# A two-layer S5 and sparse-attention trunk on one core: transposed activations, gate products and split weights placed lowest in SBUF, one 8 KB room used in turn by three stages

## The chip, the core and the metric

The program runs on one core of one Trainium2 chip. The metric is the device time of one execution in microseconds, the median of several runs. TensorE multiplies matrices, VectorE and ScalarE do elementwise work and move results out of PSUM, GpSimd (POOL) does a few small operations and issues a few DMAs, and SyncE's queue issues nearly all DMAs. SBUF, the on-chip memory, is addressed by partition (128 of them) and by a byte offset in the partition; every tile of this kernel has a range of bytes that is the same in all partitions.

## The reference

The input is 256 tokens of 1,024 float32 values. Two layers each do: half a SwiGLU block, a mixer, half a SwiGLU block. The mixer of layer 0 is an S5 state-space layer, that of layer 1 is a sparse attention with three branches, whose keys and values come from the state after layer 0. Cut to what matters here:

```
def _swiglu(x, w_in, w_out):
    a, b = jnp.split(x @ w_in, 2, axis=-1)
    return (jax.nn.silu(a) * b) @ w_out

for layer in range(2):
    h = h + 0.5 * _swiglu(_rmsnorm(h, ffn1_norm[layer]), ffn1_w_in[layer], ffn1_w_out[layer])
    u = _rmsnorm(h, mix_norm[layer])
    h = h + (_s5_mixer(u, ...) if layer == 0 else _nsa_mixer(u, kv, ...))
    h = h + 0.5 * _swiglu(_rmsnorm(h, ffn2_norm[layer]), ffn2_w_in[layer], ffn2_w_out[layer])
    if layer == 0:
        kv = _shared_kv(h, ...)
```

w_in is 1024 x 5632 and w_out 2816 x 1024. `silu(a) * b` is called the gate product below. In the attention, each branch is a softmax of logits times values; in the S5 mixer, u is multiplied into a small state per group of channels, which is scanned along the sequence.

## The kernel before

All weights stream through the core once. A load brings a *granule* of 1 MB (128 partitions x 2,048 floats) into one of two `raw` buffers. ScalarE rounds it to the 32-bit reduced float type (`whi`), VectorE takes the difference (`wlo`); each has five buffers of 4 KB per partition (lines 86 to 102). Activations are split in the same way, so that one product of float32 accuracy is three matmuls of the reduced type: high activation times high weight, high times low, low times high (`mm3`, lines 118 to 120). In these matmuls the weights are the moving operand, up to 512 columns, and the activations the stationary one, 128 x 128, loaded before each matmul.

A feed-forward block (`ffn`) runs over 11 chunks of 256 hidden columns. For a chunk, 48 matmuls multiply the transposed activations `xT` (16 KB per partition: high and low, 8 slices, 256 tokens) with w_in into the accumulators `mm`. ScalarE and VectorE form the gate product `g` from them (lines 249 and 250). In the next chunk, after its fifth slice, TensorE turns `g` (line 204), and ScalarE and VectorE write the turned product, split into high and low, to `gT` (lines 143 and 144). Then, after that chunk's own 48 matmuls, 24 matmuls multiply `gT` with w_out into the accumulators `o`, which stay for all chunks. So TensorE's order is: 48 on `xT` with four transposes after the 30th, 24 on `gT`, and so on. The four blocks are called block 1 (layer 0, first half) to block 4 (layer 1, second half). Other work is woven in where there is room: S5 preparation in block 1, attention bias tables in block 2, keys and values in block 3. `issue_after` keeps the order on each engine as written.

The S5 stage turns its normalized input into `uT` (8 KB per partition, lines 508 to 516), multiplies it with input matrices (line 527), scans (line 542), and forms the output (lines 557 to 566). Its output, split, goes into the tile `xT` again, for a product with w_glu. In the attention stage, `mix` normalizes the probabilities `Pt`, turns them 128 keys at a time (line 911), copies the turned blocks to `pt0` (ScalarE) and `pt1` (VectorE), two buffers of 2 KB each, and multiplies the values with them (line 920).

Tiles come from pools. A pool takes its bytes above the pools that are open at that time, in the order in which they were opened, and gives them back when it closes. A tile that is allocated again waits for the last user of the bytes that it gets. Open for the whole kernel are, from the bottom up: `pers` (h 8 KB, small constants, `xT` 16 KB), `rawp` (16 KB), `hip` and `lop` (20 KB each: `whi`, `wlo`), and `small`. Above them come the stage's pools: the S5 tables (104 KB) and their scratch in block 1, attention tables and scratch later, and in each block the pool `ffn`, which holds two `g` (2 KB each) and two `gT` (4 KB each). So `xT` starts 9 KB above the first pool's start, `raw` 25, `whi` 41, `wlo` 61; `gT` starts 199 KB above it in block 1, 169 KB in blocks 2 and 3, and 127 KB in block 4.

Of the kernel before, what the change touches and what calls it, by code (L numbers as in the profile page):

```python
# [9 lines left out]
F32 = mybir.dt.float32  # L10
F32R = mybir.dt.float32r
# [5 lines left out]
P = 128  # L17
D = 1024
KT = D // P
FF = 2816  # L20
CHUNKS = ((0, 4, 304), (4, 4, 256), (8, 4, 256), (12, 4, 256))
NCH = FF // 256
# [10 lines left out]
def kernel(ctx: ExitStack, tc: tile.TileContext, A, out):  # L33
    nc = tc.nc
    V, S, G, T = nc.vector, nc.scalar, nc.gpsimd, nc.tensor

    pers = ctx.enter_context(tc.tile_pool(name="pers", bufs=1))
    rawp = ctx.enter_context(tc.tile_pool(name="rawp", bufs=2))
    hip = ctx.enter_context(tc.tile_pool(name="hip", bufs=5))
    lop = ctx.enter_context(tc.tile_pool(name="lop", bufs=5))  # L40
    small = ctx.enter_context(tc.tile_pool(name="small", bufs=2))
    dscr = ctx.enter_context(tc.tile_pool(name="dscr", bufs=1, space=bass.MemoryType.DRAM))

# [5 lines left out]

    def tr_bank():  # L50
        return Banks.tr.tile([P, 512], F32, name=Banks.tag)


    h = pers.tile([P, 2, D], F32, name="h")
# [93 lines left out]
    class Acts:  # L148
        def __init__(self, hc, gain=None):
            self.h, self.gain = hc, gain  # L150
            self.xT = pers.tile([P, 2, KT, 256], F32R, name="xT")
            self.rs = small.tile([P, 2], F32, name="rs", bufs=4)
            self.ss = small.tile([P, 4], F32, name="ss")

# [36 lines left out]
    def ffn(x, gi, w_in, w_out, res, perm=False, bg=None, steps=1, done=None, first=()):  # L191
        with tc.tile_pool(name="ffn", bufs=2) as fp, tc.tile_pool(name="ps_a", bufs=1, space=PSUM) as pa:
            xT, rs = x.xT, x.rs
            acc2 = [[pa.tile([P, 512], F32, name=f"o{t}{hf}") for hf in range(2)] for t in range(2)]
            g_in = granules([w_in[c, kh] for c in range(NCH) for kh in range(2)], gain=gi, first=first)
            g_out = granules([w_out[j] for j in range(NCH)])

            def transposed(g):

                gT = fp.tile([P, 2, 2, 256], F32R, name="gT")  # L200
                ps = tr_bank()
                for f in range(2):
                    for t in range(2):
                        T.transpose(ps[:, (f * 2 + t) * P:(f * 2 + t + 1) * P], g[:, t, f * P:(f + 1) * P], ident)  # L204
                if perm:
                    src = ps.rearrange("p (f t e c) -> p f t e c", f=2, t=2, e=2)
                    hi, lo = (gT[:, i].rearrange("p f (c t e) -> p f t e c", t=2, e=2) for i in range(2))
                    for f in range(2):
                        split(hi[:, f], lo[:, f], src[:, f])
                else:  # L210
                    split(gT[:, 0], gT[:, 1], ps.rearrange("p (f c) -> p f c", f=2))
                return gT

            def second(c, gT):
                if c < NCH - 1:
                    for f in range(2):
                        for hf in range(2):
                            w = next(g_out)
                            for t in range(2):
                                mm3(acc2[t][hf], gT, f, t, w, c + f == 0, False)  # L220
                    return
                ws = [[next(g_out) for _ in range(2)] for _ in range(2)]
                for t in range(2):
                    for hf in range(2):
                        for f in range(2):
                            mm3(acc2[t][hf], gT, f, t, ws[f][hf], False, f == 1)
                        cs = slice(hf * 512, (hf + 1) * 512)
                        V.scalar_tensor_tensor(out=res[:, t, cs], in0=acc2[t][hf], scalar=0.5, in1=res[:, t, cs], op0=ALU.mult, op1=ALU.add)
                        done(t, hf)

            prev = None
            for c in range(NCH):
                acc = [mm_bank() for _ in range(2)]
                gT = None
                if c == 0:
                    gemm(acc, xT, g_in, lead=True)
                else:
                    for k in range(KT):
                        w = next(g_in)
                        for t in range(2):  # L240
                            mm3(acc[t], xT, k, t, w, k == 0, k == KT - 1)
                        if k == 4:
                            gT = transposed(prev)
                        if k % 2:
                            background(bg, steps)
                g = fp.tile([P, 2, 256], F32, name="g")
                for t in range(2):
                    sl = g[:, t, :]
                    Last.act = S.activation(sl, acc[t][:, 0:256], AF.Silu, scale=rs[:, t:t + 1])  # L249
                    Last.dve = V.scalar_tensor_tensor(out=g[:, t, :], in0=acc[t][:, 256:512], scalar=rs[:, t:t + 1], in1=sl,  # L250
                                                      op0=ALU.mult, op1=ALU.mult)
                if c:
                    second(c - 1, gT)
                prev = g
                background(bg, steps)
            second(NCH - 1, transposed(prev))

    BG1 = 1.65  # L260
    NG = 32
    NC = 64
# [221 lines left out]

    def s5(hc, x, W, kp, done):
        cosT, sinT, Cw, Wi, WBT, r4 = W.cosT, W.sinT, W.Cw, W.Wi, W.WBT, W.r4
        with tc.tile_pool(name="s5r", bufs=1) as rp, tc.tile_pool(name="s5w", bufs=2) as wp, \
                tc.tile_pool(name="ps_dr", bufs=2, space=PSUM) as pd, tc.tile_pool(name="ps_y", bufs=2, space=PSUM) as py, \
                tc.tile_pool(name="ps_g", bufs=1, space=PSUM) as pg:
            Banks.tr, Banks.tag = py, "yb"  # L490
            uT = rp.tile([P, NG, NC], F32, name="uT")
            uv = uT.rearrange("p (r a) c -> p r a c", a=2)
            yh = pers.tile([P, 2, KT, 256], F32R, name="xT")
            gacc = [[pg.tile([P, 512], F32, name=f"ga{t}{n}") for n in range(2)] for t in range(2)]
            glu_w = [load_granule(A["w_glu"][j], 512) for j in range(2)]
            gen = granules([A["w_glu"][j] for j in range(KT // 2)], first=glu_w)
# [299 lines left out]
    def attention(x, hc, done):  # L796
        with tc.tile_pool(name="at", bufs=1) as ap, tc.tile_pool(name="at2", bufs=2) as tp, \
# [8 lines left out]
            vcol = ap.tile([P, 1], F32, name="vcol")  # L806
            nc.sync.dma_start(out=vcol, in_=A["valid"])
            xT, rs = x.xT, x.rs
            rsh = ap.tile([P, 2], F32, name="rsh")
            V.tensor_scalar(out=rsh, in0=rs, scalar1=0.5, scalar2=None, op0=ALU.mult)  # L810
            qT = ap.tile([P, 16, 256], F32R, name="qT")
# [84 lines left out]
            def mix(g, t, Pt, sm):  # L896
# [9 lines left out]
                for kb in range(t + 1):  # L906
                    pts = []
                    for br in range(2):
                        ps = tr_bank()
                        for r in range(4):  # L910
                            T.transpose(ps[:, r * P:(r + 1) * P], Pt[:, r, br, kb * P:(kb + 1) * P], ident)  # L911
                        pts.append(tp.tile([P, 512], F32, name=f"pt{br}"))
                        if br:
                            V.tensor_copy(pts[br], ps)
                        else:
                            S.activation(pts[br], ps, AF.Copy)
# [198 lines left out]
```

## Time and profile before

| | before |
|---|---|
| median of three runs | 1060.9 us (1058.21 to 1061.9) |
| profiled execution | 1057.09 us |
| its span (first to last instruction) | 1055.3 us |
| TensorE (PE) busy | 996.1 us, 94% |
| VectorE, ScalarE, GpSimd busy | 669.9, 583.2, 135.8 us |
| mean granted TensorE clock | 0.982 |
| DMA | 171.73 MB, mean 163 GB/s |

A row of the page or of a group gives the line of the code, the engine, the operation, the tiles (written <- read), the number of instructions and the mean time of one. PEld is the load of a stationary operand. A row of the timeline begins with the start in microseconds from the start of the span and the duration; matmuls overlap in it, so the distance from one start to the next (the *step* below), not the duration, is what a matmul costs in a dense stretch. A row of the chain has start, duration, and what ran. A row of a stretch gives from:to, its length, then for PE, PEld, VectorE, ScalarE and GpSimd the busy time and the number of instructions, then the granted clock, the DMA engines' share and GB/s.

### The profile page before, as it was taken

Reading aid. Unit: us, or ns where it says so; the run is one execution under the profiler, and the core shown is the slowest. Engines: PE = TensorE matmul, PEld = TensorE weight load, DVE = VectorE, ACT = ScalarE, POOL = GpSimd, SP = SyncE. Lnnn points to the kernel's source line nnn. Section 1 sums busy time; section 2 is a strip of 40 time slices with the busy share of each in tenths; the row PEclk is TensorE's granted clock in tenths of the full one; section 3 lists DMA queues with packets and bytes.
Section 4 is the critical chain, followed back from the end, with each engine's and each line's share of the span. In section 5 each row is a group of like instructions: output and inputs, shape, how many; then the busy total and the mean of one; then the engine's idle time right before and its main releaser. Section 6 shows DMA issues by size and latency. Waiting matters only on the chain.

```text
span 1055.3 us, 14565 instructions
## 1 busy us (share of the span) xinstructions
PE 996.1 (94%) x5553; PEld 806.6 (76%) x5553; DVE 669.9 (63%) x1258; ACT 583.2 (55%) x1039; POOL 135.8 (13%) x142
## 2 busy tenths in 40 slices
PE   6999999988799799999999999999887999999998
PEld 5888888776577588887887888887865678888886
DVE  4999854367864556566666455555788866556553
ACT  5677675352264555554755555454876755545552
POOL 3001110327611000000013000000205210000000
PEclk9999999989899899999999999999988999999999
DMA  7556554303258755554554455553312145545551
GB/s 256 200 189 211 194 179 147 120 2 112 90 182 240 269 197 179 184 196 160 197 206 156 160 196 170 193 193 115 100 34 91 42 155 199 198 173 188 198 171 70
DMA packets 27910, 171.73 MB, mean 163 GB/s; under 512 B 4544, under 2 KB 4992, under 8 KB 9024
## 3 DMA queue, kind: packets, MB, share of 16 engines
q1 hardware_dynamic: 26192, 164.77, 45.2%
q0 software_dynamic: 1648, 6.03, 2.2%
q8 instruction: 43, 0.70, 0.3%
q14 instruction: 27, 0.22, 0.1%
HBM read 165.54 MB, written 5.24 MB: 162 GB/s over the span
## 4 chain that ended last, share of the span: by engine, by line
PE 80%; DVE 9%; ACT 4%; DMA 3%; POOL 3%; issue 1%; SPq 0%; ACTq 0%; POOLq 0%; DVEq 0%
PE mm L118 15%; PE mm L119 15%; PE mm L120 15%; PE o L118 8%; PE o L119 8%; PE o L120 8%; DMA raw<-in_w_in_dram 3%; PE tr L204 2%; DVE wlo L102 1%; DVE w L542 1%; DVE Pt L904 1%; DVE wlo L90 1%; ACT Pt L893 1%; POOL z L502 1%; PE tr L911 1%
## 5 line engine op out<-in xcount | busy, mean ns | idle before, releaser
L118 PE MATMUL mm<-whi,xT 128*128 128x512 f32 (+2 forms) x800 | 313.3, 392 | 4.0 <-ACT whi L86 2.5
L119 PE MATMUL mm<-wlo,xT 128*128 128x512 f32 (+2 forms) x800 | 306.1, 383 | 0.7 <-DVE wlo L90 0.5
L120 PE MATMUL mm<-whi,xT 128*128 128x512 f32 (+2 forms) x800 | 306.2, 383 | 0.0
L102 DVE SCALAR_TENSOR_TENSOR wlo<-raw,gains,whi 128x512 fp32r<-128x512 f32 (+2 forms) x320 | 221.4, 730 | 111.7 <-ACT whi L99 108.0
L99 ACT ACTIVATE whi<-raw,gains 128x512 fp32r<-128x512 f32 (+2 forms) x320 | 207.4, 694 | 136.1 <-PE mm L120 58.6
L90 DVE TENSOR_TENSOR wlo<-raw,whi 128x1024 fp32r<-128x1024 f32 x140 | 171.0, 1226 | 122.7 <-ACT whi L86 122.6
L86 ACT ACTIVATE whi<-raw 128x1024 fp32r<-128x1024 f32 x148 | 154.5, 1057 | 153.5 <-PE mm L120 58.2
L118 PEld LDWEIGHTS mm<-whi,xT 128*128 128x128 f32 x800 | 150.8, 189 | 35.1 <-ACT whi L86 2.9
L120 PEld LDWEIGHTS mm<-whi,xT 128*128 128x128 f32 x800 | 150.6, 188 | 29.7
L119 PEld LDWEIGHTS mm<-wlo,xT 128*128 128x128 f32 x800 | 150.9, 189 | 28.7 <-DVE wlo L90 1.5
L118 PE MATMUL o<-whi,gT 128*128 128x512 f32 x352 | 140.5, 399 | 10.9 <-ACT gT L143 10.9
L119 PE MATMUL o<-wlo,gT 128*128 128x512 f32 x352 | 139.5, 396 | 0.0
L120 PE MATMUL o<-whi,gT 128*128 128x512 f32 x352 | 138.9, 396 | 0.0
L118 PEld LDWEIGHTS o<-whi,gT 128*128 128x128 f32 x352 | 66.6, 189 | 27.6 <-ACT gT L143 12.6
L120 PEld LDWEIGHTS o<-whi,gT 128*128 128x128 f32 x352 | 66.5, 189 | 16.0 <-DVE gT L144 0.4
L119 PEld LDWEIGHTS o<-wlo,gT 128*128 128x128 f32 x352 | 66.6, 189 | 14.9
L249 ACT ACTIVATE g<-mm,rs 128x256 f32<-128x256 f32 x88 | 41.0, 471 | 28.2 <-PE mm L120 27.9
L250 DVE SCALAR_TENSOR_TENSOR g<-mm,rs,g 128x256 f32<-128x256 f32 x88 | 41.8, 481 | 22.5 <-ACT g L249 22.4
L144 DVE TENSOR_TENSOR gT<-tr,gT 128x512 fp32r<-128x512 f32 (+1 forms) x55 | 36.4, 663 | 27.4 <-ACT gT L143 27.0
L143 ACT ACTIVATE gT<-tr 128x512 fp32r<-128x512 f32 (+1 forms) x55 | 33.3, 606 | 36.1 <-PE tr L204 29.3
L140 POOL TENSOR_TENSOR rs<-ms,nhalf 128x1 f32<-128x1 f32 x12 | 7.2, 600 | 219.9 <-DVE ms L139 219.9
L893 ACT ACTIVATE Pt<-Pt,mx 128x128 f32<-128x128 f32 (+1 forms) x64 | 28.4, 445 | 6.4 <-DVE mx L888 6.4
(300 smaller groups left out, 985.2 us busy)
## 6 DMA issues: line engine op xcount, KB each, us to landing
raw<-in_w_in_dram SPq DMA_DIRECT2D x87, 1024.0 KB, 4.9
raw<-in_w_out_dram SPq DMA_DIRECT2D x44, 1024.0 KB, 4.9
raw<-in_w_kv_dram SPq DMA_DIRECT2D x6, 1024.0 KB, 4.8
raw<-in_w_glu_dram SPq DMA_DIRECT2D x4, 1024.0 KB, 4.8
raw<-in_w_o_dram SPq DMA_DIRECT2D x4, 1024.0 KB, 4.8
revd<-rev POOLq DMA_DIRECT2D x8, 384.0 KB, 16.2
raw<-in_w_qg_dram SPq DMA_DIRECT2D x6, 512.0 KB, 3.5
B<-revd POOLq DMA_DIRECT2D x1, 2048.0 KB, 10.9
```

The source lines that it names most:

```text
L86: Last.act = S.activation(hi, r, AF.Copy)
L90: Last.dve = V.tensor_tensor(out=lo, in0=r, in1=hi.bitcast(F32), op=ALU.subtract)
L99: Last.act = S.activation(hi[:, c], r[:, c], AF.Identity, scale=g_)
L102: i = V.scalar_tensor_tensor(out=lo[:, c], in0=r[:, c], scalar=g_, in1=hi[:, c].bitcast(F32), op0=ALU.mult, op1=ALU.subtract)
L118: T.matmul(ps, lhsT=xh, rhs=wh, start=start, stop=False)
L119: T.matmul(ps, lhsT=xh, rhs=wl, start=False, stop=False)
L120: Last.pe = T.matmul(ps, lhsT=xl, rhs=wh, start=False, stop=stop_)
L143: i = S.activation(dst_hi, src, AF.Copy)
L144: V.tensor_tensor(out=dst_lo, in0=src, in1=dst_hi.bitcast(F32), op=ALU.subtract)
L249: Last.act = S.activation(sl, acc[t][:, 0:256], AF.Silu, scale=rs[:, t:t + 1])
L250: Last.dve = V.scalar_tensor_tensor(out=g[:, t, :], in0=acc[t][:, 256:512], scalar=rs[:, t:t + 1], in1=sl, op0=ALU.mult, op1=ALU.mult)
L893: S.activation(Pt[:, r, br], Pt[:, r, br], AF.Exp, scale=-1.0, bias=mx[:, c:c + 1], accum_out=sm[:, c:c + 1])
```

## The change

A new pool `low` is opened first, and `hip` and `lop` right after it, so that these three lie at the bottom of SBUF; `pers`, `rawp` and all others follow above. `low` holds two tiles: `xT` (16 KB, taken out of `pers`) and `turned` (8 KB), the room. The room is used in turn:

- in a feed-forward block its two halves are the two `gT`; chunk c takes half c modulo 2. The pool `ffn` keeps only `g`;
- in the S5 stage the whole room is `uT`; the pool `s5r` is gone;
- in the attention its four quarters take the place of the two `pt0` and the two `pt1`, one after the other.

Counted from the first pool's start, `xT` lies at 0 to 16 KB afterwards, the room at 16 to 24, `whi` at 24 to 44, `wlo` at 44 to 64, `h` and the constants at 64 to 73, `raw` at 73 to 89; the other pools move up by 8 KB, since the room is counted once for all stages. No instruction is added or taken away.

```
+    low = ctx.enter_context(tc.tile_pool(name="low", bufs=1))
+    hip = ctx.enter_context(tc.tile_pool(name="hip", bufs=5))
+    lop = ctx.enter_context(tc.tile_pool(name="lop", bufs=5))
     pers = ctx.enter_context(tc.tile_pool(name="pers", bufs=1))
     rawp = ctx.enter_context(tc.tile_pool(name="rawp", bufs=2))
-    hip = ctx.enter_context(tc.tile_pool(name="hip", bufs=5))
-    lop = ctx.enter_context(tc.tile_pool(name="lop", bufs=5))
...
+    def turn_room():
+
+        return low.tile([P, 2, 1024], F32R, name="turned")
...
-            self.xT = pers.tile([P, 2, KT, 256], F32R, name="xT")
+            self.xT = low.tile([P, 2, KT, 256], F32R, name="xT")
...
             xT, rs = x.xT, x.rs
+            gTs = turn_room()
...
-            def transposed(g):
-
-                gT = fp.tile([P, 2, 2, 256], F32R, name="gT")
+            def transposed(c, g):
+
+                gT = gTs[:, c % 2].rearrange("p (i f c) -> p i f c", i=2, f=2)
...
-                            gT = transposed(prev)
+                            gT = transposed(c - 1, prev)
...
-            second(NCH - 1, transposed(prev))
+            second(NCH - 1, transposed(NCH - 1, prev))
...
-            uT = rp.tile([P, NG, NC], F32, name="uT")
+            uT = turn_room().bitcast(F32).rearrange("p b (g c) -> p (b g) c", c=NC)
...
-            yh = pers.tile([P, 2, KT, 256], F32R, name="xT")
+            yh = low.tile([P, 2, KT, 256], F32R, name="xT")
...
             xT, rs = x.xT, x.rs
+            pt_room, turn = turn_room().bitcast(F32).rearrange("p b (k c) -> p (b k) c", c=512), [0]
...
-                        pts.append(tp.tile([P, 512], F32, name=f"pt{br}"))
+                        pts.append(pt_room[:, turn[0] % 4])
+                        turn[0] += 1
```

More of the change, by code (lines that the diff above doesn't have):

```diff
@@ L486, in s5 @@
         cosT, sinT, Cw, Wi, WBT, r4 = W.cosT, W.sinT, W.Cw, W.Wi, W.WBT, W.r4
-        with tc.tile_pool(name="s5r", bufs=1) as rp, tc.tile_pool(name="s5w", bufs=2) as wp, \
+        with tc.tile_pool(name="s5w", bufs=2) as wp, \
                 tc.tile_pool(name="ps_dr", bufs=2, space=PSUM) as pd, tc.tile_pool(name="ps_y", bufs=2, space=PSUM) as py, \
```

## The prediction

> **What bounds the kernel now.** I read the page's head first: engines and the chain that ended last.
>
> ```profile
> span 1055.3 us, 14565 instructions
> PE 996.1 (94%) x5553; PEld 806.6 (76%) x5553; DVE 669.9 (63%) x1258; ACT 583.2 (55%) x1039; POOL 135.8 (13%) x142
> PE 80%; DVE 9%; ACT 4%; DMA 3%; POOL 3%; issue 1%; SPq 0%; ACTq 0%; POOLq 0%; DVEq 0%
> ```
>
> TensorE is the bound, and mostly by itself. Then I cut the span into stages, because the four feed-forward blocks and the two mixers have different limits. The next view gives busy time by stretch: the first block, the second, the last, and then the S5 stage and the attention stage.
>
> ```profile
> 36.00:150.00 114.00, 114.00 (x528) 93.80 (x527) 97.76 (x156) 81.63 (x129) 12.18 (x7) 1.00 0.57 194
> 367.00:487.00 120.00, 120.00 (x539) 98.34 (x538) 72.30 (x98) 65.32 (x98) 0.00 (x0) 1.00 0.54 185
> 867.00:1044.00 177.00, 177.00 (x793) 144.85 (x792) 99.67 (x134) 92.79 (x137) 1.12 (x2) 1.00 0.51 178
> 215.00:300.00 85.00, 68.85 (x1050) 56.01 (x1050) 63.45 (x138) 30.22 (x56) 47.06 (x45) 0.90 0.20 69
> 735.00:848.00 113.00, 96.28 (x606) 76.34 (x605) 89.42 (x343) 79.59 (x235) 29.45 (x28) 0.94 0.21 71
> ```
>
> In the blocks TensorE has no idle time and full granted clock (1.00), while VectorE, ScalarE and the DMA engines (share 0.5) have room. There the time is the number of matmuls by the step from one start to the next, and nothing else. In the two mixers TensorE idles (68.85 of 85, 96.28 of 113 us), so there a change of its step is worth less.
>
> "Busy" hides the step, since matmuls overlap in the records; it has to be read from start times. The timeline of TensorE in the last block, around one chunk:
>
> ```profile
> 942.15 0.39 PE L118 MATMUL mm<-whi,xT 128*128 128x512 f32 x1
> ...
> 946.03 0.39 PE L120 MATMUL mm<-whi,xT 128*128 128x512 f32 x1
> 946.04 0.19 PEld L118 LDWEIGHTS mm<-whi,xT 128*128 128x128 f32 x1
> 946.26 0.39 PE L118 MATMUL mm<-whi,xT 128*128 128x512 f32 x1
> ...
> 948.75 0.39 PE L120 MATMUL mm<-whi,xT 128*128 128x512 f32 x1
> ```
>
> From 946.03 to 948.75 lie 12 steps: 2.72/12 = 226.7 ns each. From 942.15 on (29 steps, 6.60 us) it is 227.6, because the first few after a switch of operand are slower. Each weight load (0.19 us) starts with the matmul before it, and the next matmul starts some 30 ns after the load's end.
>
> Now the same matmul form with the gate products (gT) as stationary operand, o<-whi,gT. In each pair the first row is the first of 24 matmuls and the second the one that follows the 24th; the pairs are of the first, the second and the last block.
>
> ```profile
> 37.27 0.39 PE L118 MATMUL o<-whi,gT 128*128 128x512 f32 x1
> 42.76 0.39 PE L118 MATMUL mm<-whi,xT 128*128 128x512 f32 x1
> ```
> ```profile
> 368.25 0.39 PE L118 MATMUL o<-whi,gT 128*128 128x512 f32 x1
> 373.86 0.39 PE L118 MATMUL mm<-whi,xT 128*128 128x512 f32 x1
> ```
> ```profile
> 953.53 0.40 PE L118 MATMUL o<-whi,gT 128*128 128x512 f32 x1
> 959.12 0.39 PE L118 MATMUL mm<-whi,xT 128*128 128x512 f32 x1
> ```
>
> 5.49, 5.61 and 5.59 us for 24: 228.8, 233.8 and 232.9 ns a step. Same operation, same shapes, same weight buffers, same accumulator pool, no idle time; what differs is where gT lies. Adding up the tile sizes of the pools that are open, gT starts about 199 KB above the first pool in block 1, 169 KB in blocks 2 and 3 (where one more pool is open below it than in block 4), and 127 KB in block 4. xT lies at 9 to 25 KB and takes 226.7. The spread is no scatter: by line, over seven runs of 24 in block 1, minimum, median and maximum agree, and over seven runs in block 2 they take a wider set of higher values.
>
> ```profile
> L118 PE MATMUL o<-whi,gT x56: 392/392/392, 37.3 to 143.2; 128*128 128x512 f32 x56
> L118 PE MATMUL o<-whi,gT x56: 392/396/400, 368.2 to 475.1; 128*128 128x512 f32 x56
> ```
>
> So the step depends on the stationary operand's place (or on something tied to it), and 227 to 228 is the best that the trace shows.
>
> **The change, part by part.** No instruction, DMA or queue position is added, removed or moved; places change, and three sets of tiles become slices of one.
>
> *Gate products into the low room.* The room starts 16 KB above the bottom and ends at 24 KB: inside the stretch that xT covers now. I take xT's settled step for gT: 24 x 226.7 = 5.44 us. Per chunk that saves 5.49-5.44 = 0.05 in block 1, 0.17 in blocks 2 and 3, 0.15 in block 4; with 11 chunks per block 0.55 + 22 x 0.17 + 1.65 = 5.9 us. With xT's mean after a switch, 227.6 (5.46 us per run), it is 5.3. TensorE has no idle time there, so it passes through; VectorE and ScalarE are idle for 14 to 48% of the same stretches, so nothing is late next. Ends: 0, if the step isn't tied to place, and 5.9. I take 5.9, the row it is nearest to being the xT row at those addresses.
>
> *xT and the split weights lower.* The forms of the two products, each at three lines alike:
>
> ```profile
> L118 PE MATMUL mm<-whi,xT 128*128 128x512 f32 x736 | 294.8, 401 | 3.9 <-ACT whi L86 2.5 <-ACT xT L143 0.7 <-DVE g L250 0.6
> L118 PE MATMUL o<-whi,gT 128*128 128x512 f32 x352 | 140.5, 399 | 10.9 <-ACT gT L143 10.9
> ```
>
> 3 x 736 = 2,208 and 3 x 352 = 1,056. xT moves from 9-25 KB to 0-16 KB, the weights from 41-81 KB to 24-64 KB. The step is flat over xT's present 16 KB and over ten weight buffers (226.7 in a run that walks over them), so I take 0. Bounds: the trace falls by 233-227 = 6 ns over some 110 KB, so 9 KB lower might give 0.5 ns on 2,208 matmuls, 1.1 us less; on the other side see the second rival.
>
> *Raw weights, h, identity and everything above shift up* (raw from 25-41 to 73-89 KB, the rest by 8 KB). What place does to ScalarE shows in one line, block 1 against block 2, whose targets lie 30 KB apart:
>
> ```profile
> L249 ACT ACTIVATE g<-mm,rs x14: 452/460/474, 38.2 to 139.9; 128x256 f32<-128x256 f32 x14
> L249 ACT ACTIVATE g<-mm,rs x15: 474/474/476, 367.8 to 486.7; 128x256 f32<-128x256 f32 x15
> ```
>
> 14 ns of 460, 3%, and part of it may have other causes. ScalarE and VectorE carry 13% of the chain, 137 us; if a third of that reads or writes shifted tiles with half such an effect, it is within 1 us either way. I take 0 and keep +-1; the S5 and branch matmuls on moved operands, in stages where TensorE idles, are within it. In the blocks that work is covered by TensorE; without cover it would be those 14 ns per instruction.
>
> *The shared room's waits.* A new user's first write waits for the last reader of the old one. S5's inputs: last reader of gT is the block's last matmul, and the writes already come after transposes that stand behind it.
>
> ```profile
> 212.66 0.24 PE o L120
> 218.18 0.23 PE yb L508 x2
> 218.44 0.29 DVE uT L514
> ```
>
> 5.5 us of slack, so 0. The last block's first gate products come a chunk after attention's last read of the turned probabilities: 0 as well.
>
> ```profile
> 855.73 0.58 PE s L920 x4
> ```
> ```profile
> L118 PE MATMUL o<-whi,gT x80: 393/396/398, 885.6 to 1043.4; 128*128 128x512 f32 x80
> ```
>
> Inside a user the halves (gT) and the four slots (probabilities) turn over as the separate buffers did, as long as dependencies are kept by part of a tile. The trace shows that they are: h is written by VectorE in one part while TensorE transposes another part.
>
> ```profile
> 736.17 0.66 PE L159 MATMUL tr<-ident,h 128*128 128x128 f32 x4
> 736.36 0.69 DVE L228 SCALAR_TENSOR_TENSOR h<-o,h 128x512 f32<-128x512 f32 x1 [0.25 <-PE o L120]
> ```
>
> Sum: -5.9 us. The profiled execution took 1057.1 us (span 1055.3 and 1.8 around it) and would take 1051.2; the median of the three runs is 1060.9 (1058.2 to 1061.9), and from there 1055.0. The three runs differ by 3.7 us, so 0.3%, 3.2 us, is about what a measurement can tell from no change.
>
> **Rivals.** *Place doesn't matter to TensorE; no change.* Then the three steps have another cause that stays, a phase between loads and matmuls that each stage falls into. For it: xT itself runs at 230 for a while after each switch, at an unchanged place. Against it: 24 matmuls in block 2 never settle, in any of seven runs. It gives 1060.9. The Trainium skill, "SBUF — State Buffer", section "Who interferes with whom", says that TensorE and ScalarE never wait on anyone and knows slowdowns only from one shared port pair; by that page the layout is worth nothing. The three step rows speak against that reading.
>
> *xT's good place is lost; slower.* All starts move, and 226.7 was seen for xT at one place only. If its 2,208 matmuls took block 1's step of 228.8, that is +4.6 us; gT at the same step would save 0 + 22 x 0.12 + 11 x 0.10 = 3.7, and the sum is 1061.8. At block 2's 233.8 it is +15.7, gT loses another 1.5, and the sum is 1078. It decides from a step of 228.5 on, where 2,208 matmuls lose what 1,056 gain. Against it: the room and xT stay in or beside the stretch where 226.7 holds.
>
> *The room is kept as one piece; slower.* Then each write of turned probabilities waits for the read before it, which takes 0.58 us:
>
> ```profile
> 780.01 0.58 PE x L920 x4
> ```
>
> Twelve pairs, 7.0 us, all in attention where TensorE idles: 1060.9 - 5.9 + 7.0 = 1062.0. For gT it would cost nothing, since one half's reader is through before the next half is written. The h rows speak against it.
>
> *Low places shorten the tail behind every weight load.* Matmuls of 304 columns on xT:
>
> ```profile
> 743.78 0.30 PE L120 MATMUL mm<-whi,xT 128*128 128x304 f32 x1
> ...
> 747.53 0.30 PE L120 MATMUL mm<-whi,xT 128*128 128x304 f32 x1
> ```
>
> 27 steps of 138.9. From 304 to 512 columns the step grows by 87.8 ns, 0.42 per column, so 512 columns alone are 216 and 11 ns are overhead. Were that gone everywhere, 2,208 x 11 + 1,056 x 17 ns = 42 us: 1019. xT's flat step over 16 KB speaks against more than a trace of it. The Trainium skill, "TensorE: Matmul & The Clock Gate", section "Back-to-back issue gap", gives N/2.4 + 2.5 ns, 216 for 512 columns, as the isolated gap; no row here of this form reaches it.
>
> **How the numbers follow.** Forecast 0.62; no effect 0.17; xT's place lost 0.10; room in one piece 0.05; tail shorter everywhere 0.03; another small loss, such as the shifted work on the other engines, 0.03. Predicted 1055.0. Within the forecast the gain is 3 to 8 us (terms of 5.3 to 5.9, 1.1 for xT, 1 either way), 1053 to 1058, widened by the runs' spread. The range that leaves out no more than 2 in 10 reaches from 1050 to 1063: it holds no effect, the room in one piece and the mild form of the lost place, not the severe one and not the shorter tail. Faster by over 0.3%: 0.64 (forecast and tail, a little lost to scatter). Within: 0.20. Slower: 0.16.
>
> **What would show it.** Right: runs of 24 o matmuls take 5.42 to 5.48 us in all blocks and spread no more from block to block; mm stays at 226 to 228; transposed copies and first writes into the room have no new releaser. Wrong: o keeps 5.6 us in blocks 2 and 3 (place is not the cause); mm steps of 229 or more (lost place); ScalarE or VectorE waiting for L920 (room in one piece); S5 or attention longer by over 1 us. A gain on TensorE that is missing in the time would show as idle time of TensorE on the splits, which is zero now.

## The result, and the profile after

The changed kernel takes 1055.22 us (median of 10 runs, 1052.88 to 1060.2) beside 1060.55 us for the kernel before (10 runs, 1057.47 to 1062.93): a ratio of 0.9956, with a 95% interval from 0.994 to 0.9971. The forecast was 1055.0 us.

The head of the page after: the span, the engines, and the chain that ended last.

```profile
span 1058.3 us, 14566 instructions
PE 999.4 (94%) x5553; PEld 814.2 (77%) x5553; DVE 672.8 (64%) x1258; ACT 584.7 (55%) x1039; POOL 134.3 (13%) x142
PE 72%; DVE 13%; DMA 5%; ACT 5%; POOL 2%; issue 2%; SPq 0%; ACTq 0%; POOLq 0%; DVEq 0%
```

The bound is the same, TensorE. This one execution took 1060.2 us, the longest of the ten, and had the lowest mean granted clock of them, 0.972, where the profile of before had 0.982; so the two spans and the shares of the chain are not to be compared, and what follows compares stages in which the clock was 1.00 in both. The next view is the busy time by stretch for the first, second and last block (columns as in the prediction: PE, PEld, DVE, ACT and POOL busy, granted clock, DMA share, GB/s).

```profile
36.00:150.00 114.00, 113.15 (x523) 92.80 (x522) 97.75 (x157) 80.83 (x129) 12.19 (x7) 1.00 0.57 194
367.00:487.00 120.00, 120.00 (x546) 99.38 (x546) 73.27 (x100) 66.76 (x100) 0.00 (x0) 1.00 0.55 190
867.00:1044.00 177.00, 177.00 (x805) 146.20 (x804) 104.30 (x141) 97.98 (x147) 1.12 (x2) 1.00 0.52 178
```

In the same 177 us of the last block 805 matmuls now start, 793 before; in 120 us of the second block 546 in place of 539. TensorE is as full there as it was and goes through its list faster. The first row shows no gain: 523 matmuls in place of 528, with 0.85 us of idle time, in which one run of 24, at 104 us, waits for its gate products. Such a wait also comes up in traces of the old layout (0.64 us at the same place with the ten places below), so it isn't put down to the change. The timeline of TensorE around three runs of 24 o matmuls, in the first, second and last block (the first row of each pair is the first of the 24, the second row the matmul that follows them):

```profile
70.17 0.39 PE L124 MATMUL o<-whi,turned 128*128 128x512 f32 x1
75.61 0.39 PE L124 MATMUL mm<-whi,xT 128*128 128x512 f32 x1
...
372.28 0.39 PE L124 MATMUL o<-whi,turned 128*128 128x512 f32 x1
377.72 0.39 PE L124 MATMUL mm<-whi,xT 128*128 128x512 f32 x1
...
957.76 0.39 PE L124 MATMUL o<-whi,turned 128*128 128x512 f32 x1
963.20 0.39 PE L124 MATMUL mm<-whi,xT 128*128 128x512 f32 x1
```

5.44 us each, 226.7 ns a step in all three blocks, where 5.49, 5.61 and 5.59 us stood. The spread inside a block is gone as well: by line, for the second block, minimum, median and maximum of one matmul's duration are now equal (392/396/400 before).

```profile
L124 PE MATMUL o<-whi,turned x56: 389/389/389, 372.3 to 477.8; 128*128 128x512 f32 x56
```

So what was forecast is what came, in the total and in each of these rows. The reason given for it was wrong all the same, as the runs show.

### The profile page after: what moved, and what is told of

The parts are those of the page before. It is cut to its first block, busy times and chain, and to the rows that moved or that the text cites. A ratio compares the mean times of both kernels' runs of the same rounds, so it can differ in the third digit from the quotient of the medians.

```text
span 1058.3 us, 14566 instructions
## 1 busy us (share of the span) xinstructions
PE 999.4 (94%) x5553; PEld 814.2 (77%) x5553; DVE 672.8 (64%) x1258; ACT 584.7 (55%) x1039; POOL 134.3 (13%) x142
## 4 chain that ended last, share of the span: by engine, by line
PE 72%; DVE 13%; DMA 5%; ACT 5%; POOL 2%; issue 2%; SPq 0%; ACTq 0%; POOLq 0%; DVEq 0%
PE mm L124 13%; PE mm L125 13%; PE mm L126 13%; PE o L124 7%; PE o L126 7%; PE o L125 7%; DMA raw<-in_w_in_dram 4%; DVE wlo L96 3%; DMA raw<-in_w_out_dram 1%; PE tr L211 1%; DVE wlo L108 1%; DVE Pt L912 1%; ACT whi L92 1%; PE dr L534 1%; DVE w L549 1%
## 5 line engine op out<-in xcount | busy, mean ns | idle before, releaser
L124 PE MATMUL o<-whi,turned 128*128 128x512 f32 x352 | 139.1, 395 | 8.0 <-ACT turned L149 8.0
L126 PE MATMUL o<-whi,turned 128*128 128x512 f32 x352 | 137.7, 393 | 0.6 <-DVE turned L150 0.6
L125 PE MATMUL o<-wlo,turned 128*128 128x512 f32 x352 | 138.0, 392 | 0.0
L124 PEld LDWEIGHTS o<-whi,turned 128*128 128x128 f32 x352 | 66.7, 190 | 23.4 <-ACT turned L149 10.1
L126 PEld LDWEIGHTS o<-whi,turned 128*128 128x128 f32 x352 | 66.6, 189 | 15.4 <-DVE turned L150 1.4
L125 PEld LDWEIGHTS o<-wlo,turned 128*128 128x128 f32 x352 | 66.7, 189 | 13.6
L150 DVE TENSOR_TENSOR turned<-tr,turned 128x512 fp32r<-128x512 f32 (+1 forms) x55 | 36.4, 663 | 27.4 <-ACT turned L149 27.0
L149 ACT ACTIVATE turned<-tr 128x512 fp32r<-128x512 f32 (+1 forms) x55 | 33.5, 609 | 33.7 <-PE tr L211 26.7
```

Source lines behind the costliest of these rows:

```text
L124: T.matmul(ps, lhsT=xh, rhs=wh, start=start, stop=False)
L125: T.matmul(ps, lhsT=xh, rhs=wl, start=False, stop=False)
L126: Last.pe = T.matmul(ps, lhsT=xl, rhs=wh, start=False, stop=stop_)
L149: i = S.activation(dst_hi, src, AF.Copy)
L150: V.tensor_tensor(out=dst_lo, in0=src, in1=dst_hi.bitcast(F32), op=ALU.subtract)
```

## The experiments

Two theories were set against each other. **Place**, the prediction's: the step of a matmul depends on how far from the bottom of SBUF its stationary operand lies. **Distance**: it depends on the start address of the stationary operand minus that of the moving one (the split weights), counted modulo a small power of two. The addresses follow from the tile sizes in the order of allocation. In the kernel before, xT and all the split weights start 224 bytes past a multiple of 512 from the first pool (xT after h, identity, gains and a small constant: 8,928 = 17 x 512 + 224), and gT starts 160, 320, 320 and 32 bytes past one in blocks 1 to 4: 448, 96, 96 and 320 bytes ahead of the weights modulo 512. In the changed kernel xT (16 KB), the room (8 KB) and ten buffers of 4 KB stand one behind another from the bottom, so all of them are in line. The change moved gT down and, as a by-product, into line with the weights.

Since a span depends on the clock, stages tell more. This table is worked out from start times of matmuls in the traces: a block from its first o matmul to its last, attention from block 3's last o to block 4's first mm matmul, in us. Half clock is the time in which the granted clock was 0.5; blocks 1, 3 and 4 have none, block 2 has it between its first and third run of 24 o matmuls.

```
                          before  after  again  room  xT,weights  gT padded (two runs)
block 1                   176.60 177.52 176.11 177.76   178.11     176.42 176.09
block 3                   179.10 177.08 177.07 178.78   178.88     177.23 177.21
block 4                   165.25 163.21 163.18 165.06   164.97     163.27 163.27
block 2, first to second
  run of o                 25.10  26.37  26.72  24.99    25.74      26.14  25.83
block 2, first to third    43.48  45.67  46.51  43.97    44.22      45.65  45.19
  of it at half clock       6.83  10.24  13.65   6.83     6.83      10.24  10.24
block 2, third to last    132.53 130.98 130.94 132.30   132.48     131.04 131.05
attention                 122.88 127.43 125.41 123.81   126.49     123.89 123.88
  of it at half clock      13.65  23.89  17.07  17.07    20.48      17.07  17.07
```

**The changed kernel once more**, to have its gain a second time and a trace at a better clock (0.978).

> The changed kernel once more, for a second profile beside the others on one chip. Place theory (the step of a matmul hangs on where its stationary operand lies): about 1055, ratio 0.994 to 0.997 to the kernel before, o runs of 24 in 5.44 us in all four blocks, mm unchanged at 226 to 228. A profiled execution with fewer half-clock windows than the first one should have a span near 1052.

1056.25 us (1055.26 to 1058.83) beside 1059.46 for before: ratio 0.9974 [0.9962, 0.9986]. The two estimates of the gain are 4.7 and 2.8 us; both are gains, the second just short of the expected ratio. The span of its trace is 1054.7 us, where one near 1052 was expected.

**The room alone lowered.** It lies at the very bottom, 0 to 8 KB; xT, raw and the split weights keep their order above it.

```diff
+    low = ctx.enter_context(tc.tile_pool(name="low", bufs=1))
     pers = ctx.enter_context(tc.tile_pool(name="pers", bufs=1))
     rawp = ctx.enter_context(tc.tile_pool(name="rawp", bufs=2))
...
+            gTs = turn_room()
...
-            uT = rp.tile([P, NG, NC], F32, name="uT")
+            uT = turn_room().bitcast(F32).rearrange("p b (g c) -> p (b g) c", c=NC)
```

> Only the 8 KB room lies lowest; xT, raw, whi and wlo follow in the order of before, 8 KB higher (xT at 17 to 33 KB, whi and wlo at 49 to 89). Place theory: o at 226.7 in every block, mm at 226.7, time as the changed kernel (ratio 0.994 to 0.997). Distance theory (the step hangs on the difference of the start addresses of stationary and moving operand modulo 512 bytes, which is 0 for xT in both kernels and for the room only in the changed one): the difference is 224 here, o stays at 231 to 234, no gain (ratio 0.999 to 1.001). Theory that all low places count: less than the whole gain, since weights lie higher than in the changed kernel.

1059.12 us, ratio 1.0006 [0.9991, 1.0021]. A run of 24 o matmuls in its last block:

```profile
971.98 0.39 PE L124 MATMUL o<-whi,turned 128*128 128x512 f32 x1
977.57 0.39 PE L124 MATMUL mm<-whi,xT 128*128 128x512 f32 x1
```

5.59 us, 233 ns a step, at the lowest place there is. The whole mechanism of the prediction falls with these two rows. The room stands 288 bytes out of line with the weights here. The run also shows that sharing the room costs nothing that its interval could tell (0.9 us less to 2.2 us more).

**xT and the split weights alone lowered.** gT, uT and the turned probabilities stay where they were, to the byte.

```diff
-    pers = ctx.enter_context(tc.tile_pool(name="pers", bufs=1))
-    rawp = ctx.enter_context(tc.tile_pool(name="rawp", bufs=2))
+    low = ctx.enter_context(tc.tile_pool(name="low", bufs=1))
     hip = ctx.enter_context(tc.tile_pool(name="hip", bufs=5))
     lop = ctx.enter_context(tc.tile_pool(name="lop", bufs=5))
+    pers = ctx.enter_context(tc.tile_pool(name="pers", bufs=1))
+    rawp = ctx.enter_context(tc.tile_pool(name="rawp", bufs=2))
```

> The rest of the change alone: xT at 0 to 16 KB, whi and wlo at 16 to 56 KB, but gT, S5 inputs and turned probabilities in separate tiles at the addresses of before. Place theory: o steps as before (about 229, 234, 234, 233 in blocks 1 to 4), time as before (ratio 0.999 to 1.001). Distance theory: gT against whi differs by other amounts than before (160, 320, 320 and 32 bytes in blocks 1 to 4), so block 1 becomes slower (about 233) and block 4 near 227 to 228. Theory that all low places count: part of the gain here (ratio 0.997 to 0.999).

1062.33 us, ratio 1.0036 [1.0023, 1.0049]: slower. The same form in the same block 1, with gT at the same address as before:

```profile
L119 PE MATMUL o<-whi,gT x56: 394/394/399, 36.4 to 143.4; 128*128 128x512 f32 x56
```

392/392/392 before. The operand has not moved and its step rose from 229 to 233.2 ns, because the weights moved by a number of bytes that isn't a multiple of 512. Between this run and the one before it, place is refuted from both sides. One expectation of the distance theory missed: block 4, 32 bytes from the line here, was to come near 227 to 228 ns and took 233.1, so being near the line doesn't help. The steps explain only part of the 2.9 us: in block 1 they are worth 11 x 24 x 4.4 ns, 1.2 us, in blocks 3 and 4 they give back 0.5 us (table), and by the table most of the rest lies in attention, which is taken up below.

**Ten places in block 4**, used in turn, from 82 to 199 KB above the first pool, 13 KB apart, all with the same distance modulo 512. The attention tables are given up before the block to make room, and each unused tile between two places gets one short write of VectorE's.

```diff
+                for n in range(10):
+                    places.append(fp.tile([P, 2, 2, 256], F32R, name=f"gT{n}", bufs=1))
+                    if n < 9:
+                        pad = fp.tile([P, 2304], F32, name=f"pad{n}", bufs=1)
...
-                gT = fp.tile([P, 2, 2, 256], F32R, name="gT")
+                gT = places[c % 10] if scan else fp.tile([P, 2, 2, 256], F32R, name="gT")
```

> The kernel before, but in block 4 the attention tables are given up first and each chunk has a gT of its own, from 82 KB above the first pool's start in steps of 13 KB to 199 KB, all with the same start modulo 512 bytes. Place theory: the step changes from chunk to chunk, about 233 at 121 to 134 KB, 234 at 173, 229 at 199; 82 to 108 KB unknown, between 226.7 and 233. Distance theory: all ten places take one step, about 233.

1058.95 us in one run. The settled step is 233.3 to 233.4 ns at all ten places, over 117 KB of address.

**gT put into line where it is.** Nothing is lowered; an unused tile of 64, 416, 416 and 192 bytes stands ahead of gT in blocks 1 to 4.

```diff
-    def ffn(x, gi, w_in, w_out, res, perm=False, bg=None, steps=1, done=None, first=()):
+    def ffn(x, gi, w_in, w_out, res, perm=False, bg=None, steps=1, done=None, first=(), skip=0):
...
+            fp.tile([P, skip // 4], F32, name="skip", bufs=1)
```

> The kernel before with an unused tile of 64, 416, 416 and 192 bytes ahead of gT in blocks 1 to 4, so that gT starts at the same address modulo 512 bytes as the split weights; nothing is lowered, gT stays 130 to 204 KB above the bottom. Distance theory (the step of a matmul depends on the start address of its stationary operand minus that of its moving one, modulo 512 bytes): the o matmuls of all four blocks step at 226.7 to 227 ns as the mm matmuls do, blocks 3 and 4 lose 1.7 to 2.1 us each, the whole 4 to 6 us: 1055 to 1057 us beside 1060.5 for before, a ratio of 0.995 to 0.997; if the eighth blocked VectorE multiply of attention is an accident of the lowered layout it stays away and the ratio is at the lower end. Place theory (the prediction's): no step changes, 1060.5, ratio 1.000.

1054.07 us, ratio 0.9923 [0.9896, 0.995]. A run of the second block:

```profile
386.71 0.39 PE L118 MATMUL o<-whi,gT 128*128 128x512 f32 x1
392.15 0.39 PE L118 MATMUL mm<-whi,xT 128*128 128x512 f32 x1
```

5.44 us with gT 170 KB up. In the table its blocks 3 and 4 are within 0.2 us of the changed kernel's. Four pads do all that the new layout does for TensorE; the whole gained more than the 0.995 to 0.997 that was expected. The same text a second time:

> The same text as the run with gT in line in all four blocks, beside the run above on the same chip, to see whether padding alone beats the changed kernel: 1053.5 to 1056 us, ratio 0.992 to 0.996; 27.0 us of Pt<-Pt,sm and 122 to 124 us of attention.

1053.5 us, ratio 0.9948 [0.9932, 0.9964].

**xT put out of line, and lowered.** xT moves from 9 KB above the first pool to 320 bytes above it, 96 bytes out of line with the weights; the rest keeps its place modulo 512.

```diff
+    pers.tile([P, 80], F32, name="skip0")
+    xt_room = pers.tile([P, 2, KT, 256], F32R, name="xT")
+    pers.tile([P, 48], F32, name="skip1")
     h = pers.tile([P, 2, D], F32, name="h")
```

> The kernel before with xT moved to the lowest KB of SBUF (16 KB from 320 bytes above the bottom) and 96 bytes out of line with the split weights modulo 512 bytes; the weights, gT and oT keep their places modulo 512. Distance theory: the mm matmuls, the 2,208 with 512 columns that have xT as their stationary operand, step at 233 to 234 ns in place of 226.7, so 2,208 x 6.5 to 7.3 ns = 14 to 16 us more: 1075 to 1077 us, ratio 1.013 to 1.016; less only where a stage waits for its weights by DMA (block 2's start). Place theory: xT stands lower than before, so no step grows and the time is 1060.5 or a little less, ratio 0.999 to 1.000.

1071.69 us, ratio 1.0108 [1.0079, 1.0138]. Place has no answer to this; distance forecast 14 to 16 us and got 11.4 (8.4 to 14.6 by the interval). Two rows of the last block, 29 steps apart, as the prediction had them for before:

```profile
940.33 0.39 PE L121 MATMUL mm<-whi,xT 128*128 128x512 f32 x1
...
947.12 0.39 PE L123 MATMUL mm<-whi,xT 128*128 128x512 f32 x1
```

6.79 us in place of 6.60, 234.1 ns a step in place of 227.6. The forecast took the settled 226.7 as its start; from the mean of before, 228.0 over the whole trace, 2,208 x 6.0 ns are 13.3 us, which lies inside the interval. Where the rest stays was not measured; chunks that wait for their weights may hide it.

**The offsets one by one.** Ten gT tiles in block 4, used in turn, 0 to 288 bytes ahead of the weights in steps of 32, and eight more offsets in block 3.

```diff
+            for n, skip in enumerate(skips):
+                if skip:
+                    fp.tile([P, skip // 4], F32, name=f"skip{n}", bufs=1)
+                places.append(fp.tile([P, 2, 2, 256], F32R, name=f"gT{n}", bufs=1))
...
-                gT = fp.tile([P, 2, 2, 256], F32R, name="gT")
+                gT = places[c % len(places)] if skips else fp.tile([P, 2, 2, 256], F32R, name="gT")
```

> The kernel before with ten gT tiles in block 4 and eight in block 3, used in turn, that start at 0, 32, 64, 96, 128, 160, 192, 224, 256 and 288 bytes (block 4) and 320, 352, 384, 416, 448, 480, 0 and 256 bytes (block 3) past the split weights' start, modulo 512. Each tile serves one or two runs of 24 o matmuls. Distance theory: 226.7 to 227 ns at offset 0 in both blocks, some 229 at 448, 233 to 234 at 32, 96, 160, 288 and 320, some 232 at 384; the others are not known, and show whether the step is a matter of lying in line or grows with the distance. If the period were 256 bytes, offset 256 would be as fast as 0. Place theory: in each block the step grows or stays from tile to tile with the address, without regard to the offset. The whole stays within 2 us of before.

Four runs of block 4, at 0, 96, 192 and 256 bytes, in order of time and of address:

```profile
888.04 0.39 PE L118 MATMUL o<-whi,gT 128*128 128x512 f32 x1
893.48 0.39 PE L118 MATMUL mm<-whi,xT 128*128 128x512 f32 x1
...
938.80 0.39 PE L118 MATMUL o<-whi,gT 128*128 128x512 f32 x1
944.42 0.39 PE L118 MATMUL mm<-whi,xT 128*128 128x512 f32 x1
...
989.76 0.39 PE L118 MATMUL o<-whi,gT 128*128 128x512 f32 x1
995.26 0.39 PE L118 MATMUL mm<-whi,xT 128*128 128x512 f32 x1
...
1023.58 0.39 PE L118 MATMUL o<-whi,gT 128*128 128x512 f32 x1
1029.02 0.39 PE L118 MATMUL mm<-whi,xT 128*128 128x512 f32 x1
```

5.44, 5.62, 5.50 and 5.44 us. The whole took 1058.88 us in one run, beside one run of before with 1063.97 at a granted clock of 0.973: more than the 2 us that were expected, in too few runs to say what it means; before's medians elsewhere, 1059.46 to 1060.55, are within them. All offsets, each from one run of 24 in the same way (ns a step):

```
offset, bytes      0     32     64     96    128    160    192    224    256    288
block 4         226.7  233.1  233.3  233.9  232.9  233.3  228.9  233.0  226.7  233.1
offset, bytes    320    352    384    416    448    480      0    256
block 3         233.3  234.0  232.9  233.3  228.9  233.0  226.7  226.7
```

Block 3's row repeats block 4's at 256 bytes less in every place, within 0.1 ns: at these multiples of 32 bytes the step is a function of the distance modulo 256. The run with xT and the weights lowered, whose weights start 224 bytes elsewhere, has three of these distances, 160, 64 and 32, and the same steps: 233.2, 233.3 and 233.1. So it is the difference that counts, not either address. It doesn't grow with the distance; of eight offsets one is free, one (192) costs 2.2 ns, and six cost 6 to 7. A distance of 128, half of 256, is no better than the rest (232.9). Block 1 of the kernel before happened to stand at 448, that is 192, and its other blocks at 96 and 64; that is the whole of the 228.8, 233.8 and 232.9 which the prediction read as a slope over place.

**oT in line as well**, by 128 bytes ahead of it in the padded kernel, and by 416 in the changed kernel.

```diff
+            ap.tile([P, 32], F32, name="skip0")
             oT = ap.tile([P, 2, KT, 256], F32R, name="oT")
+            ap.tile([P, 96], F32, name="skip1")
```

> As the run before last (gT in line with the split weights in all four blocks), and oT, the stationary operand of attention's output matmuls, put in line as well by 128 unused bytes ahead of it. Distance theory: oT's matmuls step at 226.7 ns in place of some 232, so 0.4 to 0.6 us less than with gT in line alone; 1054.5 to 1056.5 us, ratio 0.994 to 0.9965. Place theory: 1060.5, ratio 1.000.

> The changed kernel with 416 unused bytes ahead of oT, which puts oT in line with the split weights; all else as in the changed kernel. Distance theory: oT's matmuls step at 226.7 ns in place of 232 to 234, 0.4 to 0.7 us less than the changed kernel: 1054.5 to 1055.5 us. Place theory: as the changed kernel, 1055.2 to 1056.3. If the eighth blocked VectorE multiply in attention hangs on an accident of the order in time, it may come or go here too, worth about 1 us.

1054.71 us, ratio 0.9941 [0.9919, 0.9964], and 1056.3 us, 0.9956 [0.9942, 0.997]. The mean of oT's undisturbed steps (from one oT matmul to the next in under 260 ns, 65 to 72 of 96) falls from 232.7 to 228.9 ns in the first and from 233.7 to 229.2 in the second, some 0.3 us, less than either interval can show: the step falls, its median to 227 ns, and the time is inconclusive. The second time is 0.8 us above the end of its range. The changed kernel had moved oT from 128 to 96 bytes out of line, from 232.8 to 233.7 ns.

**What attention gives back.** The table has attention 2.5 and 4.6 us longer in the two traces of the changed kernel. Part of that goes with the clock. At the same 17.07 us of half clock it is 125.4 against 123.8 and 123.9 with only the room lowered or gT padded, some 1.5 us more. One group of instructions shows 1 us of it: VectorE's multiplies by the row scale, in the view by groups of the stretch from 735 to 862 us, of before, after, with gT padded, and in the run described next (busy us in the stretch, mean ns of one, idle).

```profile
L904 DVE TENSOR_SCALAR Pt<-Pt,sm 128x128 f32<-128x128 f32 (+1 forms) x64 | 24.0, 422 | 0.2
```
```profile
L912 DVE TENSOR_SCALAR Pt<-Pt,sm 128x128 f32<-128x128 f32 (+1 forms) x64 | 25.0, 438 | 0.2
```
```profile
L906 DVE TENSOR_SCALAR Pt<-Pt,sm 128x128 f32<-128x128 f32 (+1 forms) x64 | 23.9, 421 | 0.2
```
```profile
L915 DVE TENSOR_SCALAR Pt<-Pt,sm 128x128 f32<-128x128 f32 (+1 forms) x64 | 25.0, 438 | 0.2
```

64 x 422 ns is 27.0 us, 64 x 438 is 28.0. The extra microsecond is one multiply. The timelines of VectorE and GpSimd at the same moment, first of before, then of the changed kernel's second trace:

```profile
812.32 1.67 DVE L904 TENSOR_SCALAR Pt<-Pt,sm 128x128 f32<-128x128 f32 x3
...
813.74 5.08 POOL L95 TENSOR_TENSOR wlo<-raw,whi 128x512 fp32r<-128x512 f32 x4 [0.23 <-ACT whi L86]
```
```profile
812.49 2.74 DVE L912 TENSOR_SCALAR Pt<-Pt,sm 128x128 f32<-128x128 f32 x3
...
813.88 4.96 POOL L101 TENSOR_TENSOR wlo<-raw,whi 128x512 fp32r<-128x512 f32 x4 [0.20 <-ACT whi L92]
```

Before, three multiplies are through in 1.67 us, at 813.99, soon after GpSimd's pause of 0.23 us; in the changed kernel the three take 2.74 us, because one more of them missed the pause, here of 0.20 us, and lasts 1.35 us, about as long as a subtraction of GpSimd's (1.27 us). In each trace seven or eight of the 64 are held up so (over 600 ns): eight in all five traces with xT and the weights lowered, seven in all eight without. The pause goes with it in all thirteen: 205 to 215 ns where eight are held up, 221 to 239 where seven are. Was it that the weights no longer start in line with raw, from which they are split? **The changed kernel 224 bytes higher**, so that xT, the room, the split weights and raw are all in line:

```diff
+    skip = ctx.enter_context(tc.tile_pool(name="skip", bufs=1))
+    low.tile([P, 56], F32, name="skip0")
+    skip.tile([P, 72], F32, name="skip1")
```

> The changed kernel with 224 unused bytes below xT and 288 above the split weights: xT, the room and the split weights keep their low places but start at 352 modulo 512 bytes, where the raw weights start (in the changed kernel they start at 128, 224 bytes out of line with raw). The step theory (only stationary against moving counts): o and mm stay at 226.7 to 227 ns. Two theories of the time given back in attention: if it comes from the splits being out of line with raw, the VectorE multiplies Pt<-Pt,sm go from 28.0 us back to 27.0, the stage between block 3's last o and block 4's first mm matmul from 125.4 to 127.4 back to 122 to 124, and the whole to 1053 to 1055 us; if it comes from the low place itself or from an accident of order, 28.0 us, 125 to 127 and 1055 to 1056.5 stay.

1054.44 us, ratio 0.9956 [0.9937, 0.9974]; the multiplies stay at 28.0 us (the last of the four rows above). So alignment with raw isn't what holds up the eighth multiply; whether the low place does it or a shift of some 20 ns in the order of events is open. The other half microsecond is open too, and here alignment with raw isn't ruled out: attention takes 125.2 us with 20.48 us of half clock, where the runs with xT and the weights lowered and with oT in line, at the same half clock, take 126.5 and 126.9. That is not the 122 to 124 that were expected if alignment with raw counted, but the whole came out in the range expected for that case (1053 to 1055 us).

## Why the prediction was right, and where it was not

*The sum, -5.9 us: right in size in the first measurement.* Measured -5.3 between the medians of the ten runs (-4.7 by the ratio), but only -2.8 by the ratio of the repeat. The second sum, "5.3" with xT's mean of 227.6, is a slip: 1,056 matmuls at 0.9 ns more take 1.0 us off, so it is 5.0.

*Gate products into the low room: the size of the term was right, the reason wrong.* The step that failed is the sentence "So the step depends on the stationary operand's place". The three values, 228.8, 233.8 and 232.9, were ordered by a kind of height only if one didn't mind that 199 KB was faster than 169 and 127 KB; that was the sign that height isn't the variable. What the runs showed in its place: the distance to the moving operand modulo 256 bytes, 226.7 ns a step at 0, and 228.9, 233.9 and 233.3 at the 192, 96 and 64 that the blocks had before. The bracket "(or on something tied to it)" kept the door open without a price, and the rival "place doesn't matter" was priced at no change because it assumed that a cause other than place would stay. It did not: this change happens to lay five sets of tiles, all multiples of 4 KB, one behind another. That gT came to 226.7 ns was therefore luck. By the table of offsets, one unused tile of 32 bytes between the room and the weights would have put the room and xT at 224, at 233.0 ns a step: no gain on gT, and a loss on xT's 2,208 matmuls (an estimate, not run). The room alone, 288 bytes out of line, shows the first half of that.

*By block: right where TensorE is full.* Per run of 24 the savings are 0.05, 0.17 and 0.15 us, as worked out. Blocks 3 and 4 return 2.0 us each (table), where 22 x 0.17 / 2 = 1.9 and 1.65 were forecast; the mm matmuls behind each o run settle faster too (in block 4 their first six steps take 231.5 ns on average before and 226.7 after; the mean over the trace falls from 228.0 to 227.6). Block 1 returns 0.5 us of the forecast 0.55 in the repeat, whose trace has no wait there. Block 2 returns 1.6 us from its third run to its last, where nine times 0.17, 1.5 us, was forecast. What the prediction left out is block 2's opening, where TensorE is not full. The view of the waits between 300 and 353 us, before and in the second trace of the changed kernel (total us, times, longest):

```profile
ACT whi L99 <- DMA raw<-in_w_in_dram: 15.8, 2, 8.5
PE o L118 <- ACT gT L143: 7.5, 1, 7.5
```
```profile
ACT whi L105 <- DMA raw<-in_w_in_dram: 17.4, 2, 9.5
PE o L124 <- ACT turned L149: 9.7, 1, 9.7
```

ScalarE, which splits the weights and writes the gate products in one queue, waits for the weights themselves, and longer than before. From its first run of o to its third, block 2 takes 43.48 us before and 45.67 and 46.51 in the two traces of the changed kernel, so that the block as a whole gives back more than it gained. That loss goes with the half clock, not with the layout alone: it is 6.83 us before and 10.24 and 13.65 after. At 6.83 us the padded kernel with oT in line takes 43.63 us, and at 10.24 us the kernel with the ten offsets, whose block 2 is that of before, takes 45.49. Whether the longer wait brings the longer half clock or the other way round is open.

At equal clock the steps are thus worth some 6 us (0.5, 1.6, 2.0 and 2.0), as forecast, and attention takes 1.5 us of it back, which leaves about 4.5: near the first measurement's 4.7, above the repeat's 2.8. The pads alone, whose attention takes no longer than that of the room alone, gained 8.2 and 5.5 us by the ratios of their two measurements.

*xT and split weights lower, 0: right here, for the other reason.* They moved by the same number of bytes modulo 256 and stayed in line. The rival "xT's good place is lost" was a true danger with a wrong trigger: at a step of 233.8 it was priced at +15.7, and xT out of line cost 11.4.

*Shifted work of ScalarE and VectorE, 0 and +-1: missed a little.* Attention gives back about 1.5 us at equal clock, half a microsecond more than the bound, which was one of the prediction's own signs of being wrong. 1 us of it is VectorE's hold-up behind GpSimd, which the prediction didn't look at. The 14 ns between blocks 1 and 2 in ScalarE's activation stay as they were: it reads 453/462/480 and 477/477/478 ns now.

*The room's waits, 0: right.* The writers of the turned probabilities wait for nothing but their transposes, as before:

```profile
DVE turned L923 <- PE tr L919: 3.4, 6, 0.9
```
```profile
DVE pt L914 <- PE tr L911: 2.9, 6, 0.7
```

No wait for their readers (L929 after the change) appears, so the room is kept by parts; S5's first write into it, at 218.6 us, comes 4.5 us after the last o matmul started.

*The shorter tail everywhere:* no group of o or mm matmuls settled below 226.7 ns in any run, at any place or offset.

## What to carry to other kernels

When two groups of equal matmuls step at different rates with nothing waiting, write down the start addresses of both operands of each group before forming a theory, and look at their difference modulo 256 bytes. Here, with 128 x 128 against 128 x 512 operands, being in line was worth 6 to 7 ns of 234 on a matmul at most distances, 3% where TensorE sets the pace, and four pads of at most 416 bytes bought it without a new layout: 1053.5 to 1054.1 us, at least as good as the changed kernel's 1055.2 to 1056.3. Compare stages at the same granted clock: block 2's opening looks like a loss through the layout until its half clock is counted. A forecast that comes out right on three rows has not tested its reason; one row that varies the suspected cause alone has.

## What the runs showed of the hardware that was not expected

- The step of a 512-column matmul with its weight load depends on (start of stationary - start of moving) modulo 256 bytes: 226.7 ns at 0, 228.9 at 192, 232.9 to 234.0 at the six other multiples of 32 (two blocks, 18 offsets), at starts from 0 to 203 KB above the first pool. Why the period is 256 bytes, and why 192 is nearly as good as 0, is open; offsets between the multiples of 32 were not run.
- The transposes' step (128 columns, 108 to 109 ns) didn't change with the layout.
- A VectorE multiply of 0.24 to 0.35 us lasts 1.2 to 1.5 us while GpSimd subtracts. Whether one more of them slips through goes with a pause of GpSimd's, 205 to 215 or 221 to 239 ns, in all thirteen traces.
- Block 2's first three runs of o take 43.5 to 44.2 us with 6.83 us of half clock, 45.2 to 45.7 with 10.24, in both cases with gT in line and out of it, and 46.5 in the one trace with 13.65.
